# Order of declaration in a constant pool: the token rows ahead of the short vectors

## The chip, the cores and the metric

The kernel runs on one core of one Trainium2 chip. The metric is the device time of one execution in microseconds (us); lower is better. A core has five engines that work through their own instruction streams in order: TensorE (PE in the profile, with its weight loads shown apart as PEld), VectorE (DVE), ScalarE (ACT), GpSimd (POOL) and SyncE (SP, which here only starts DMA transfers). [...]

## The reference

A trunk of two layers over 512 tokens of width 1024 in float32. Each layer is a token mixer and a gated feed-forward block, each behind an RMS norm and added to the residual:

```python
for i in range(2):
    h = rms_norm(x, norm_mix[i])
    x = x + (mixer_a if i == 0 else mixer_b)(h, ...)
    h = rms_norm(x, norm_ffn[i])
    x = x + conv_ffn(h, f_w_up[i], f_conv_w[i], f_conv_b[i], f_w_down[i])
return rms_norm(x, norm_final)
```

`mixer_a` is a chunked causal gMLP (`gelu(h @ w_in)` split into u and v, v normed and mixed over the tokens of a chunk, `(u * v) @ w_out`); `mixer_b` a Griffin RG-LRU block (two projections, a short convolution, two gates, a linear recurrence, a projection out). `conv_ffn` is `(gelu(gate) * val) @ w_down` with `gate, val = split(causal_dwconv(h @ w_up))`, a convolution of width 3 over the tokens. The feed-forward width is 3072.

## The kernel before, in words

Everything is kept transposed: channels on the 128 partitions, the 512 tokens along the row. `xall` holds the residual x as 8 rows of 128 x 512 numbers (`xs[0]` to `xs[7]`). A product is made accurate by splitting both factors into a high and a low part of type fp32r. The gain-scaled x is kept so as `xh[0..7]` and `xl[0..7]`, eight tiles of 128 x 512 each (`norm_input`, L210 to L213); the weights are loaded in pieces of 128 x 1024 numbers (`raw`), and ScalarE makes the high part (L99), VectorE the low part (L100), each in a ring of three buffers of pool `wp`. One product is then three matmuls (`mm3`, L109 to L113): high by high, high weight by low x, low weight by high x.

In a TensorE matmul one factor of 128 x 128 is loaded first (the stationary one, a row of PEld) and the other, here 512 columns, streams past it (the moving one). The order in which the program runs, and what stands in each role:

- **v** (L374 to L376): four blocks of 96 matmuls. Here `xh` and `xl` are the stationary factor, 128 columns of them at a time, and the weights stream.
- **u** (four blocks of 96, the groups named `u` in the trace): the weights are stationary, `xh` and `xl` stream. In between stand the short matmuls `sv` that mix the tokens of a chunk.
- **aop** (384 matmuls): projection out of mixer A; the streaming factor is `ayh`/`ayl`, tiles of pool `yp`.
- **f** (12 blocks of 96 in each of two layers, named `f`, weights `fu...`): up-projection of the feed-forward block, `xh` and `xl` stream.
- **d** (L522): the first part of the down-projection by seven products of half size with 256 columns each; tiles `y` stream. In layer 0 twice 504 such matmuls, in layer 1 once, and there the rest is an ordinary projection (**fd**, L269 ff.), also over tiles `y`.
- **bx, bg** (three blocks of 96 each): `xh` and `xl` stream; in between stand the gate products **gt** (24 matmuls per head, streaming `xbh`/`xbl` of pool `yp`).
- **bop** (288 matmuls): projection out of mixer B, streaming `byh`/`byl` of pool `yp`.

So `xh` and `xl` are used in v, u, f, bx and bg, and in nothing else. The normalising factor of a token is not applied to x before the product but to the result: VectorE multiplies each finished 128 x 512 block by `rbc` (L545 in f, L448 in u, L631 and L642 in bx and bg). `acc` collects the squares for the norm (L221), TensorE sums it over the partitions (L232), and L246 spreads the factor over a 128 x 512 block that ScalarE copies to `rbc` (L247).

`vt` holds all short vectors (gains, convolution taps, biases) side by side, 536 columns; single columns of it are operands of ScalarE and VectorE instructions. The tiles of pool `const` get their addresses in the order in which they are declared, one behind the other, each size rounded up to 32 bytes. In the program that is built, `const` begins at byte 16512 of each partition, a multiple of 64, for `vt` takes 2144 bytes, which is 33 times 64 and 32 more: `xall` begins at byte 18656, 32 beyond a multiple of 64, and so do the sixteen tiles behind it (2048 bytes each). `acc` and `rbc`, declared at L203 and L204, begin at 69920 and 71968, 32 beyond a multiple of 64 too. Every tile of the other pools (weights, `ay`, `by`, `xb`, `y`, work tiles) begins on a multiple of 64.

The order of the work is set by a scheduler at build time, which gives each engine one fixed list; `tc.high_priority` (the weight splits and a few others) moves work ahead in it.

Of the kernel before, what the change touches and what calls it, by code (L numbers as in the profile page):

```python
# [8 lines left out]
F32 = mybir.dt.float32  # L9
# [5 lines left out]
P = 128  # L15
S = 512
# [24 lines left out]
NV = _off  # L41
# [3 lines left out]
def trunk(ctx: ExitStack, tc: tile.TileContext, xT, vecs, a_w_in, a_w_sT, a_b_s, a_w_out,  # L45
# [3 lines left out]
    const = ctx.enter_context(tc.tile_pool(name="const", bufs=1))  # L49
# [41 lines left out]
    def small(n, name):  # L91
        return const.tile([P, n], F32, name=name)
# [42 lines left out]
        return f  # L135


    vt = const.tile([P, NV], F32, name="vt")
    xall = const.tile([P, KD, S], F32, name="xall")
    xs = [xall[:, k, :] for k in range(KD)]  # L140
    xh = [const.tile([P, S], F32R, name=f"xh{k}") for k in range(KD)]
    xl = [const.tile([P, S], F32R, name=f"xl{k}") for k in range(KD)]
    xparts = list(zip(xh, xl))
    g0 = const.tile([P, KD], F32, name="g0")
    nc.scalar.dma_start(g0, vecs[:, _COLS["norm_mix"]:_COLS["norm_mix"] + KD])

# [53 lines left out]
        nc.vector.tensor_scalar(c4, u, LRU_C / 2, None, op0=ALU.mult)  # L200


    acc = const.tile([P, S], F32, name="acc")  # L203
    rbc = const.tile([P, S], F32, name="rbc")  # L204
    rc = small(NC, "rc")
    ms = small(NC, "ms")
    rch = const.tile([P, NC], F32R, name="rch")
# [560 lines left out]
```

## Time and profile before

| what | before |
|---|---|
| median of 3 runs | 1327.69 us (1327.13 to 1328.07) |
| the profiled execution | 1328.25 us, of which the span of the core is 1326.5 us |
| TensorE clock granted over the span | 0.998 of full speed |
| PE busy | 1316.4 us (99%), 6510 matmuls |
| PEld busy | 1103.5 us (83%) |
| DVE busy | 935.2 us (71%) |
| ACT busy | 600.6 us (45%) |
| POOL busy | 54.3 us (4%) |
| DMA | 143.47 MB, mean 108 GB/s |

"Busy" is the time in which an engine has at least one instruction under way. Matmuls overlap: the record of a 128 x 512 matmul is about 0.4 us long while the next one starts after 0.23 us, so what one costs in a stream is read from the distance of starts, not from its own length. The chain of waits is followed back from the last instruction: to whatever released each step, or to the instruction before it on its engine.

### The profile page before, as it was taken

How to read it: one execution, taken by the hardware profiler on the slowest of the kernel's cores; microseconds unless marked ns; L12 is line 12 of the kernel's file. 1: busy time of each engine (PE TensorE's matmuls, PEld its weight loads, DVE VectorE, ACT ScalarE, POOL GpSimd, SP SyncE). 2: the span in 40 equal slices, each digit the busy share in tenths (PEclk: the TensorE clock that was granted, in tenths of full speed). 3: DMA queues.
4: the chain of work that ended last, by engine and by line, in shares of the span. 5: the costliest groups of instructions: out<-in, count | busy, mean ns of one | idle time of the engine just before them, and what ended most of it. 6: DMA issues, size and time to landing. Idle time of an engine off the chain costs nothing.

```text
span 1326.5 us, 17029 instructions
## 1 busy us (share of the span) xinstructions
PE 1316.4 (99%) x6510; PEld 1103.5 (83%) x6510; DVE 935.2 (71%) x1336; ACT 600.6 (45%) x809; POOL 54.3 (4%) x56
## 2 busy tenths in 40 slices
PE   9999999999999999999999999999999999999997
PEld 7888888888888898888997888888888899888886
DVE  7227776446777877878987799954687788576735
ACT  6456333333444443444554669633344444343432
POOL 1000000000000120001200000000000012000000
PEclk9999999999999999999999999999999999999999
DMA  6333222232223574225752323233222357322221
GB/s 231 96 95 111 81 80 80 95 97 95 95 96 94 124 188 130 89 92 130 178 137 96 96 80 95 96 111 96 84 91 96 111 135 182 113 95 96 96 80 64
DMA packets 121105, 143.47 MB, mean 108 GB/s; under 512 B 7616, under 2 KB 95168, under 8 KB 121024
## 3 DMA queue, kind: packets, MB, share of 16 engines
q1 hardware_dynamic: 111088, 132.95, 31.5%
q0 software_dynamic: 9792, 9.44, 4.7%
q8 instruction: 51, 0.84, 0.3%
q14 instruction: 30, 0.25, 0.1%
q10 hardware_dynamic: 144, 0.00, 0.0%
HBM read 140.26 MB, written 2.10 MB: 107 GB/s over the span
## 4 chain that ended last, share of the span: by engine, by line
PE 99%; issue 1%; DVE 0%; DVEq 0%; POOLq 0%; POOL 0%
PE f L111 14%; PE f L112 14%; PE f L113 14%; PE v L374 2%; PE d000m L522 2%; PE d001m L522 2%; PE v L375 2%; PE u L111 2%; PE d101m L522 2%; PE d061m L522 2%; PE d100m L522 2%; PE d060m L522 2%; PE u L113 2%; PE u L112 2%; PE v L376 2%; PE aop L111 2%
## 5 line engine op out<-in xcount | busy, mean ns | idle before, releaser
L458 DVE SCALAR_TENSOR_TENSOR cv<-up,vt,cv 128x511 f32<-128x511 f32 x192 | 135.8, 745 | 0.7
L545 DVE TENSOR_TENSOR up<-f,rbc 128x512 f32<-128x512 f32 x96 | 63.7, 686 | 35.6 <-PE f L113 33.2
L456 ACT ACTIVATE cv<-up,vt 128x512 f32<-128x512 f32 x96 | 70.7, 804 | 0.5 <-DVE up L545 0.5
L561 ACT ACTIVATE cv<-cv 128x512 f32<-128x512 f32 x48 | 30.3, 632 | 34.4 <-DVE cv L458 34.3
L502 DVE TENSOR_TENSOR y<-yr,y 128x1792 fp32r<-128x1792 f32 x18 | 36.5, 2025 | 11.8 <-ACT y L501 11.8
L501 ACT CAST y<-yr 128x1792 fp32r<-128x1792 f32 x18 | 30.4, 1691 | 14.3 <-DVE yr L499 14.3
L226 POOL TENSOR_TENSOR rc<-ms,mhalf 128x4 f32<-128x4 f32 (+1 forms) x6 | 5.5, 912 | 665.2 <-DVE ms L225 665.2
L434 DVE SCALAR_TENSOR_TENSOR sv<-sv,vt,bs 128x256 f32<-128x256 f32 x32 | 15.0, 478 | 19.1 <-PE sv L431 19.1
L211 ACT ACTIVATE xh<-xall,vt 128x512 fp32r<-128x512 f32 x24 | 17.1, 717 | 20.3 <-DVE xall L263 15.8
L220 ACT ACTIVATE sq<-xall 128x512 f32<-128x512 f32 (+1 forms) x37 | 21.5, 586 | 9.8 <-DVE xall L275 9.8
L563 DVE TENSOR_TENSOR yr<-cv 128x512 f32<-128x512 f32 x36 | 24.7, 688 | 1.7
L458 DVE SCALAR_TENSOR_TENSOR xb<-xr,vt,xb 128x511 f32<-128x511 f32 (+2 forms) x36 | 25.5, 744 | 0.1
L221 DVE TENSOR_TENSOR acc<-acc,sq 128x512 f32<-128x512 f32 (+1 forms) x37 | 23.8, 642 | 2.0 <-ACT sq L220 1.9
L212 DVE SCALAR_TENSOR_TENSOR xl<-xall,vt,xh 128x512 fp32r<-128x512 f32 x24 | 17.8, 747 | 3.4 <-ACT xh L211 3.2
L430 PE MATMUL sv<-ws,vh 128*128 128x256 f32 x64 | 15.4, 324 | 0.0
L436 DVE SCALAR_TENSOR_TENSOR sv<-sv,vt 128x256 f32<-128x256 f32 x32 | 15.0, 479 | 0.4
L567 ACT CAST y<-cv 128x512 fp32r<-128x512 f32 x12 | 7.3, 617 | 16.1 <-DVE cv L565 16.1
L431 PE MATMUL sv<-ws,vl 128*128 128x128 f32 x64 | 14.2, 223 | 0.0
L698 DVE TENSOR_TENSOR_SCAN hs<-riyh,sq 128x512 f32<-128x512 f32 x12 | 14.0, 1207 | 0.0
L86 ACT ACT_TABLE_LOAD x10 | 12.8, 1283 | 0.1
L497 DVE TENSOR_TENSOR yr<-yr 128x512 f32<-128x512 f32 x18 | 12.5, 692 | 0.6
L431 PEld LDWEIGHTS sv<-ws,vl 128*128 128x128 f32 x64 | 12.3, 192 | 0.5
(2631 smaller groups left out, 4505.7 us busy)
## 6 DMA issues: line engine op xcount, KB each, us to landing
xall<-xT SPq DMA_DIRECT2D x8, 256.0 KB, 5.3
outT<-o SPq DMA_DIRECT2D x8, 256.0 KB, 2.2
av00raw<-a_w_in SPq DMA_DIRECT2D x2, 256.0 KB, 4.3
av01raw<-a_w_in SPq DMA_DIRECT2D x2, 256.0 KB, 5.6
av02raw<-a_w_in SPq DMA_DIRECT2D x2, 256.0 KB, 5.8
av03raw<-a_w_in SPq DMA_DIRECT2D x2, 256.0 KB, 4.8
bs<-a_b_s SPq DMA_DIRECT2D x1, 512.0 KB, 5.9
av10r<-a_w_in SPq DMA_DIRECT2D x1, 512.0 KB, 6.0
```

What stands on the lines that cost most here:

```text
L111: nc.tensor.matmul(ps, wh, xh, start=first, stop=False)
L112: nc.tensor.matmul(ps, wh, xl, start=False, stop=False)
L113: nc.tensor.matmul(ps, wl, xh, start=False, stop=last)
L374: nc.tensor.matmul(pss[c], xh[kk][:, ts], hi[:, k, :], start=kk == 0, stop=False)
L375: nc.tensor.matmul(pss[c], xh[kk][:, ts], lo[:, k, :], start=False, stop=False)
L456: nc.scalar.activation(dst, src, AF.Identity, scale=col(wname, woff + last * wstep), bias=col(cname, coff))
L458: nc.vector.scalar_tensor_tensor(dst[:, i:], src[:, :S - i], col(wname, woff + (last - i) * wstep), dst[:, i:], op0=ALU.mult, op1=ALU.add)
L501: nc.scalar.copy(hi, raw[:, 0:7])
L502: nc.vector.tensor_tensor(lo, raw[:, 0:7], hi.bitcast(F32), op=ALU.subtract)
L522: nc.tensor.matmul(banks[b][:, j], wt[:, w, js], xt, start=first and j == 0 and m == 0, stop=last and j == 1 and m == 2, skip_group_check= ...
L545: nc.vector.tensor_tensor(upt, pss[2 * half + j], rbc, op=ALU.mult)
L561: nc.scalar.activation(ts[0], ts[0], AF.Gelu_apprx_tanh)
```

## The change

Inside the constant pool, `vt` is declared behind the rows instead of ahead of them, and `acc` and `rbc` are declared with the rows instead of behind the small vectors. No instruction is added, removed or written otherwise.

```diff
-    vt = const.tile([P, NV], F32, name="vt")
+
     xall = const.tile([P, KD, S], F32, name="xall")
     xs = [xall[:, k, :] for k in range(KD)]
     xh = [const.tile([P, S], F32R, name=f"xh{k}") for k in range(KD)]
     xl = [const.tile([P, S], F32R, name=f"xl{k}") for k in range(KD)]
     xparts = list(zip(xh, xl))
+    acc = const.tile([P, S], F32, name="acc")
+    rbc = const.tile([P, S], F32, name="rbc")
+    vt = const.tile([P, NV], F32, name="vt")
     g0 = const.tile([P, KD], F32, name="g0")
...
-    acc = const.tile([P, S], F32, name="acc")
-    rbc = const.tile([P, S], F32, name="rbc")
     rc = small(NC, "rc")
```

In the built program the lists of instructions of all five engines are the same as before, row for row, with the same waits; only addresses differ:

| tile | byte in the partition, before | after |
|---|---|---|
| `xall` | 18656 = 291 x 64 + 32 | 16512 = 258 x 64 |
| `xh0` | 35040 = 547 x 64 + 32 | 32896 = 514 x 64 |
| `xl0` | 51424 = 803 x 64 + 32 | 49280 = 770 x 64 |
| `acc` | 69920 = 1092 x 64 + 32 | 65664 = 1026 x 64 |
| `rbc` | 71968 = 1124 x 64 + 32 | 67712 = 1058 x 64 |
| `vt` | 16512 = 258 x 64 | 69760 = 1090 x 64 |
| `ones`, the stationary factor of L246 | 68352 = 1068 x 64 | 72448 = 1132 x 64 |
| first tile of the next pool, `wp` | 74304 = 1161 x 64 | 74304, the same |

The other `xh` and `xl` follow in steps of 2048 bytes. From `rc` on, nothing moves.

## Rows read from the trace of the kernel before

**Rows 1.** The page: span, busy time by engine, the chain that ended last.
```profile
span 1326.5 us, 17029 instructions
PE 1316.4 (99%) x6510; PEld 1103.5 (83%) x6510; DVE 935.2 (71%) x1336; ACT 600.6 (45%) x809; POOL 54.3 (4%) x56
...
PE 99%; issue 1%; DVE 0%; DVEq 0%; POOLq 0%; POOL 0%
```

**Rows 2.** The waits, those of PE: waited for, us in total, times, longest us.
```profile
PE rb L298 <- DVE dg L291: 1.5, 1, 1.5
PE warm L158 <- DVE warm L155: 1.3, 1, 1.3
PE st L287 <- ACT sq L277: 1.0, 1, 1.0
```

**Rows 3.** Busy time of u, bg, f, v, bop, gt, from start to start.
```profile
core 0: us, PE busy (x) PEld busy (x) DVE busy (x) ACT busy (x) POOL busy (x), PEclk, DMA share, GB/s
97.45:119.94 22.49, 22.49 (x97) 18.11 (x96) 18.89 (x29) 17.91 (x32) 1.01 (x1) 1.00 0.36 113
829.24:851.73 22.49, 22.49 (x97) 18.11 (x96) 22.49 (x33) 13.70 (x19) 0.00 (x0) 1.00 0.28 95
940.86:963.35 22.49, 22.49 (x98) 18.12 (x96) 17.63 (x23) 9.86 (x11) 0.00 (x0) 1.00 0.29 94
52.65:75.05 22.40, 22.40 (x97) 18.03 (x96) 4.90 (x4) 9.63 (x17) 0.00 (x0) 1.00 0.29 93
851.73:917.03 65.30, 65.30 (x289) 54.10 (x288) 35.20 (x46) 25.83 (x35) 0.00 (x0) 1.00 0.32 105
801.46:806.90 5.44, 5.44 (x26) 4.51 (x24) 5.44 (x10) 5.41 (x8) 0.00 (x0) 1.00 0.39 103
```

**Rows 4.** Busy time over the span of the instructions with `xh`, then with `xl`.
```profile
0.00:1326.00 1326.00, 773.31 (x2432) 458.91 (x2432) 23.84 (x32) 22.84 (x32) 1.00 0.37 108
0.00:1326.00 1326.00, 481.99 (x1216) 229.37 (x1216) 23.84 (x32) 1.00 0.37 108
```

**Rows 5.** Groups by line, DVE and ACT, whole span: busy us, mean ns of one.
```profile
L545 DVE TENSOR_TENSOR up<-f,rbc 128x512 f32<-128x512 f32 x96 | 63.7, 686 | 35.6 <-PE f L113 33.2
L563 DVE TENSOR_TENSOR yr<-cv 128x512 f32<-128x512 f32 x36 | 24.7, 688 | 1.7
...
L212 DVE SCALAR_TENSOR_TENSOR xl<-xall,vt,xh 128x512 fp32r<-128x512 f32 x24 | 17.8, 747 | 3.4 <-ACT xh L211 3.2
L400 DVE SCALAR_TENSOR_TENSOR vl<-vr,rv,vh 128x512 fp32r<-128x512 f32 x16 | 10.9, 745 | 1.9 <-ACT vh L399 1.9
...
L399 ACT ACTIVATE vh<-vr,rv 128x512 fp32r<-128x512 f32 x16 | 10.1, 711 | 1.5 <-POOL rv L226 1.5
L211 ACT ACTIVATE xh<-xall,g 128x512 fp32r<-128x512 f32 x8 | 5.7, 715 | 2.2 <-DMA xall<-xT 1.1 <-DMA g<-vecs 1.0
```

**Rows 6.** One weight tile of an f block: its low part written (DVE), then loaded (PEld).
```profile
L113 PEld LDWEIGHTS f<-xh,fu122l x8: 187/188/193, 974.8 to 979.8; 128*128 128x128 f32 x8
L100 DVE TENSOR_TENSOR fu122l<-fu122r,fu122h x1: 1225/1225/1225, 964.4 to 964.4; 128x1024 fp32r<-128x1024 f32 x1
```

**Rows 7.** Busy time by stretch: the whole of the three bg blocks.
```profile
762.40:851.70 89.30, 89.30 (x385) 72.27 (x384) 88.67 (x128) 67.21 (x91) 0.00 (x0) 1.00 0.28 89
```

**Rows 8.** Timeline, PEld, in layer 0's first d stage and the first bg block.
```profile
455.38 0.19 PEld L522 LDWEIGHTS d000m<-y,d0001blo 128*128 128x128 f32 x1 [0.21 <-DVE d0001blo L483]
...
772.25 0.19 PEld L111 LDWEIGHTS gt<-xb4h,gw2h 128*128 128x128 f32 x1 [0.16 <-DVE xr L631]
```

**Rows 9.** Timeline, PE and DVE, in the first bx block and at the last one's end.
```profile
682.00 0.39 PE L111 MATMUL bx<-xh,bx00h 128*128 128x512 f32 x1
...
695.46 0.69 DVE L221 TENSOR_TENSOR acc<-acc,sq 128x512 f32<-128x512 f32 x1
...
696.51 0.28 PE L232 MATMUL st<-ones_f,acc 128*128 128x1 f32 x2
...
759.56 1.28 DVE L631 TENSOR_TENSOR xr<-bx,rbc 128x512 f32<-128x512 f32 x2
```

## The prediction

> **What bounds the kernel now.** I read the page first, for the engine that is the bound. TensorE is at work 99% of the span, and 99% of the chain that ended last is TensorE's [rows 1]. The waits come second: all of PE's add up to 3.8 us, and all three stand at the start or in the last 17 us [rows 2]. So between the first chunk and the tail, the time is the number of matmuls times the distance of their starts. The change takes no matmul away; it can only alter that distance, or the length of the work on VectorE and ScalarE beside it.
>
> So the third view is the distance in different stretches, each taken from the start of a first matmul to the start of the next stretch's first one, divided by the weight loads in it (one per matmul) [rows 3]:
>
> - one block each of u, bg and f, where `xh` and `xl` stream: 22.49 us / 96 = 234.3 ns in all three;
> - a block of v, where `xh` and `xl` are stationary and weights stream: 22.40 / 96 = 233.3 ns;
> - bop, streaming tiles of pool `yp`: 65.30 / 288 = 226.7 ns;
> - the gt of one head, inside a bg block, streaming such tiles: 5.44 / 24 = 226.7 ns.
>
> All are 128 x 512 with fp32r operands at a granted clock of 1.00, the 2.4 GHz level, where 512 columns take 213.3 ns. What the stretches at 233 and 234 ns share is `xh` or `xl`, which begin 32 bytes beyond a multiple of 64; every operand of the two at 226.7 ns begins on one. How busy the neighbours are does not sort them: v is at 233.3 ns with VectorE busy 4.90 of 22.40 us, gt at 226.7 ns with VectorE busy all of 5.44 us, and bg's own matmuls, with VectorE just as busy, at 234.3 ns [rows 3]. The surplus, 7.5 ns and 6.6 ns, is 18 and 16 columns at 2.4 GHz; 64 bytes hold 16 numbers. A row that starts off the boundary touching one more piece of 64 bytes would look like this. I take the address for the cause.
>
> **The change part by part.**
>
> *Streaming `xh` and `xl` on 64 bytes.* 2432 matmuls use `xh` and 1216 `xl`, 3648 in all [rows 4]; 4 x 96 = 384 are v's, so 3264 stream them: 2304 in f, 384 in u, 576 in bx and bg. Their price afterwards is not in the trace. Its ends are 234.3 ns (the address does nothing) and 226.7 ns (they become like bop). I take 226.7, as the same helper, shape and types run there. 3264 x 7.6 ns = 24.7 us (22.49/96 less 65.30/288, unrounded, is 7.54: 24.6 us).
>
> *Stationary `xh` and `xl` in v.* The ends are 0 and 384 x (233.3 - 226.7) = 2.5 us. I take 2.5: nothing but these operands is off the boundary in v either, and its surplus is nearly the same. This is the less certain term, as a weight load lies beside the matmul ahead of it.
>
> *`xall`, `acc`, `rbc` and `vt`, read and written by VectorE and ScalarE: nothing.* Pairs of rows with the same work differ by at most 4 ns, with either sign: with `rbc` off the boundary 686 ns, all on it 688; `xl` out of `xall` 747, `vl` 745; `xh` 715, `vh` 711 [rows 5]. Were the 4 ns real, the work would still lie beside TensorE, which is the bound. If that cover went, 96 x 4 ns for a group such as L545 would be 0.4 us.
>
> *What is given back.* The lists and waits stay, so an earlier TensorE can only run into what is late. In an f block VectorE works 17.63 us [rows 3], and a block would take 96 x 226.7 = 21.77 us: still room. A low weight part there is written by 965.6 and first loaded at 974.8, 9.2 us ahead [rows 6]; the whole gain of a block is 0.72 us. Four places are tight, two of them in the first bx block:
>
> - Layer 0's first d stage already waits for VectorE, 0.21 us [rows 8]. VectorE's chain of weight sums starts off buffers that TensorE frees in the f block ahead, so it moves along with TensorE; what TensorE can gain on it lies between nothing and the 0.72 us of that block. I take 0.2.
> - In the first bx block the last sum for the norm ends at 696.15, 0.36 us ahead of L232 [rows 9]. From the block's start at 682.00 to there stand some 60 matmuls, 0.45 us: 0.1 lost. The 12 matmuls from there to L246 lose another 0.1 us, for the chain over VectorE and GpSimd between has its own length.
> - In the first bg block, gt waits 0.16 us for VectorE to empty a bank of PSUM [rows 8], and VectorE works 88.67 of 89.30 us in the bg blocks [rows 7]. The emptying of those banks began at 759.56 [rows 9], 12.7 us earlier; they hold some 55 matmuls, 24 of them gt, so 31 of bg: up to 0.2 us.
>
> I take 0.6 us for all four; the ends are 0 and 2.2 us (VectorE holds TensorE to its own pace through all three bg blocks: 288 x 7.5 ns).
>
> *Sum.* 24.6 + 2.5 - 0.6 = 26.5 us. The profiled execution took 1328.25 us for a span of 1326.5, so it would take 1301.75. It stands 0.56 us above the median of the three runs, 1327.69; for the median that is **1301.2 us**.
>
> **The rivals.**
>
> 1. *Only the streaming operand counts.* Then v keeps its 233.3 ns for another reason (it alone has the roles exchanged). For: weight loads are 188 ns long [rows 6] and lie beside the running matmul. Against: the surplus is 16 columns, as in f. The sum loses 2.5 us: 1303.7 us.
>
> 2. *VectorE takes over in the second half.* In bx and bg the 576 matmuls of these blocks would gain 4.3 us, but VectorE has 0.63 us of idle time in the bg blocks [rows 7]. If it is the bound from the last bx block on, 2.2 us (bg) to 4.3 us (bx and bg) of the gain are lost: 1303.4 to 1305.5 us. Against: PE has no wait in these blocks that the list of waits counts [rows 2], and the one in the timeline is 0.16 us [rows 8]; in the last of them, with VectorE at work all the time, TensorE still runs at 234.3 ns [rows 3].
>
> 3. *The address does nothing.* What sets `xh` and `xl` apart is then something else that moves with them unchanged (that they are written by ScalarE and VectorE at the end of a stage, or read by five stages). The distances stay at 234.3 and 233.3 ns and the time at 1327.7 us. Against: `ayh`, `byh` and `xbh` are written in the same way, by one ScalarE and one VectorE instruction each. The Trainium skill has a rule that speaks for this rival: "SBUF — State Buffer", section "Specifications (TRN2)", gives lines of 16 bytes as the unit in which reads pay for crossing over. By that, a row that starts 32 bytes beyond a multiple of 64 starts on a line as well as after the change, and the sum would be 0. By that rule, v, f, u, bx and bg should run as bop does, and the rows disagree by 6.6 and 7.5 ns.
>
> 4. *Slower: the neighbours pay.* TensorE's streams, VectorE and ScalarE now all begin in the same phase of 64 bytes, and VectorE's instructions in the f blocks become longer because they meet TensorE's reads. The place is VectorE in f: it decides from 22.49 / 17.63, 28% longer instructions, on; at 30% a block takes 22.9 us, 24 blocks lose 24 x 0.43 = 10 us, and the time is 1338 us. Against: L563, with all its operands on the boundary, takes 688 ns in the same stage, L545 686 [rows 5].
>
> **How the numbers follow.** About 0.2% (2.7 us) is what a measurement of this kernel can tell from no change. My forecast gets 0.77, rival 1 0.09, rival 2 0.06, rival 3 0.05, rival 4 0.03. Forecast and rivals 1 and 2 are faster by over 1.6%: faster 0.92, same 0.05, slower 0.03. The forecast's own range runs from 1300.6 (all of 27.1 us, nothing given back) to 1302.8 (all of 2.2 given back); the runs of before spread by 0.9 us, so the low end is 1299.8. For the high end, rivals 1 and 2 belong in, up to 1305.5 and the spread: 1306. Rivals 3 and 4, 0.08, are left out.
>
> **What would show it.** Right: blocks of f, u, bx and bg of 21.8 us and of v of 21.8 us, bop unchanged at 65.3; the d stages, fd and the tail as long as before; instructions of VectorE and ScalarE of the same length. TensorE's busy time falls with the span and its share stays at 99%. Blocks of v at 22.4 show rival 1. New waits of PE for VectorE in bg, or bg blocks longer than those of f by more than their gt, show rival 2. Blocks of f at 22.5 show rival 3 and make the prediction wrong, as would an L545 longer than its 686 ns by a fifth.

## The result, and the profile after

| | before | after |
|---|---|---|
| median, runs of one chip | 1327.76 us (1327.13 to 1328.07, 4 runs) | 1311.65 us (1311.40 to 1314.92, 4 runs) |
| ratio | | 0.9885, 95% interval 0.9868 to 0.9902 |
| the profiled execution | 1328.25 us, span 1326.5 | 1311.40 us, span 1309.7 |

Faster, by 16.1 us, where 26.5 us were forecast and 1306 us was the high end of the range. The sign was right; 10.4 us of the gain are missing. The page of the profile after, against [rows 1]:

```profile
span 1309.7 us, 17029 instructions
PE 1299.0 (99%) x6510; PEld 1100.3 (84%) x6510; DVE 934.5 (71%) x1336; ACT 600.8 (46%) x809; POOL 54.3 (4%) x56
...
PE 98%; issue 1%; DMA 0%; DVE 0%; ACT 0%; DVEq 0%; POOLq 0%; POOL 0%
```

PE's busy time fell by 17.4 us and the span by 16.8; VectorE and ScalarE work as long as before, within 0.7 us. TensorE is still the bound. So the gain did not run into another engine: the matmuls themselves gained less than forecast. Their distance stands in the same stretches as in [rows 3], in the same order (u, bg, f, v, bop, gt; columns as there):

```profile
core 0: us, PE busy (x) PEld busy (x) DVE busy (x) ACT busy (x) POOL busy (x), PEclk, DMA share, GB/s
96.72:119.12 22.40, 22.40 (x97) 18.16 (x96) 18.89 (x29) 17.81 (x32) 1.01 (x1) 1.00 0.36 112
818.45:840.42 21.97, 21.97 (x97) 18.04 (x96) 21.97 (x32) 13.65 (x19) 0.00 (x0) 1.00 0.30 97
929.14:951.12 21.98, 21.98 (x98) 18.04 (x96) 17.64 (x23) 9.90 (x11) 0.00 (x0) 1.00 0.30 96
51.92:74.33 22.41, 22.41 (x98) 17.96 (x97) 4.90 (x4) 9.62 (x17) 0.00 (x0) 1.00 0.31 93
840.42:905.75 65.33, 65.33 (x289) 54.08 (x288) 36.41 (x48) 25.84 (x35) 0.00 (x0) 1.00 0.32 105
790.96:796.45 5.49, 5.49 (x26) 4.51 (x24) 5.49 (x10) 5.46 (x8) 0.00 (x0) 1.00 0.36 99
```

f and bg went from 234.3 to 228.9 ns (21.97 / 96), this block of u only to 233.3, and v stayed at 233.4. None reached the 226.7 ns of bop (65.33 / 288 = 226.8), though all their operands now begin on 64 bytes. The gt shown takes 0.05 us more than before: by the trace its first ten matmuls, right behind those of bg, start 224 to 236 ns apart, the others every 226.7 ns. The clock is 1.00 in all of them.

By the starts of the stages, the 16.8 us between the two spans (16.9 before rounding) lie as follows: 0.7 ahead of u, 1.4 from u's start to aop's, 0.0 in aop, 6.7 from layer 0's first f block to bx (12 blocks of f at 0.51 us are 6.1 of it), 1.2 in bx with the gt between, 1.4 in bg, and 5.6 from bop's start to the end (again 12 blocks of f, less 0.5 us that the stretch from fd's start to the end is longer, 78.3 us after 77.8). The 0.7 us ahead of u are no gain of v's stream: they lie in v's first block, where the program starts up (24.1 us before, 23.4 after); the other three blocks take 22.95, 22.40 and 22.40 us in both kernels.

The waits of PE are those of [rows 2] and one more, in v's beginning; the lines of VectorE and ScalarE last as long as in [rows 5]:

```profile
PE rb L299 <- DVE dg L292: 1.5, 1, 1.5
PE warm L161 <- DVE warm L158: 1.3, 1, 1.3
PE st L288 <- ACT sq L278: 1.0, 1, 1.0
PE v L375 <- ACT av00hi L356: 0.6, 1, 0.6
```

```profile
L546 DVE TENSOR_TENSOR up<-f,rbc 128x512 f32<-128x512 f32 x96 | 63.6, 686 | 32.8 <-PE f L113 31.0
L564 DVE TENSOR_TENSOR yr<-cv 128x512 f32<-128x512 f32 x36 | 24.7, 687 | 1.7
...
L213 DVE SCALAR_TENSOR_TENSOR xl<-xall,vt,xh 128x512 fp32r<-128x512 f32 x24 | 17.8, 746 | 3.4 <-ACT xh L212 3.2
```

One more view says what sort of thing the missing time is. The timeline after, PE, grouped by weight tile, in u's second block and in an f block: smallest, median and largest length in ns, then the starts of the first and the last one in us. The lengths are modelled, but from matmul to matmul their differences are clear:

```profile
L111 PE MATMUL u<-xh,au10h x8: 397/398/398, 119.1 to 124.0; 128*128 128x512 f32 x8
L112 PE MATMUL u<-xl,au10h x8: 397/398/398, 119.4 to 124.3; 128*128 128x512 f32 x8
L113 PE MATMUL u<-xh,au10l x8: 397/398/398, 119.6 to 124.5; 128*128 128x512 f32 x8
L111 PE MATMUL u<-xh,au11h x8: 393/394/448, 125.6 to 130.5; 128*128 128x512 f32 x8
L112 PE MATMUL u<-xl,au11h x8: 388/388/397, 125.9 to 130.7; 128*128 128x512 f32 x8
L113 PE MATMUL u<-xh,au11l x8: 392/392/393, 126.1 to 130.9; 128*128 128x512 f32 x8
...
L111 PE MATMUL f<-xh,fu111h x8: 394/394/395, 934.6 to 939.4; 128*128 128x512 f32 x8
L112 PE MATMUL f<-xl,fu111h x8: 388/388/389, 934.9 to 939.7; 128*128 128x512 f32 x8
L113 PE MATMUL f<-xh,fu111l x8: 392/392/392, 935.1 to 939.9; 128*128 128x512 f32 x8
```

Up to 124.5 us every matmul is long, in u's first block too. Then the short `sv` matmuls come in between, and from 125.6 us on the same stream, over the same addresses, has a pattern of three, which the blocks of f have too. So a row that begins on 64 bytes doesn't settle the pace by itself: something beside it does, and it can stand in more than one state.

### The profile page after: what moved, and what is told of

Same layout as the page of the kernel before. It is cut to its first block, busy times and chain, and to the rows that moved or that the text cites. A ratio compares the mean times of both kernels' runs of the same rounds, so it can differ in the third digit from the quotient of the medians.

```text
span 1309.7 us, 17029 instructions
## 1 busy us (share of the span) xinstructions
PE 1299.0 (99%) x6510; PEld 1100.3 (84%) x6510; DVE 934.5 (71%) x1336; ACT 600.8 (46%) x809; POOL 54.3 (4%) x56
## 4 chain that ended last, share of the span: by engine, by line
PE 98%; issue 1%; DMA 0%; DVE 0%; ACT 0%; DVEq 0%; POOLq 0%; POOL 0%
PE f L111 14%; PE f L112 13%; PE f L113 13%; PE v L375 2%; PE d101m L523 2%; PE d061m L523 2%; PE d001m L523 2%; PE d100m L523 2%; PE d000m L523 2%; PE d060m L523 2%; PE v L376 2%; PE u L111 2%; PE v L377 2%; PE u L112 2%; PE u L113 2%; PE aop L111 2%
## 5 line engine op out<-in xcount | busy, mean ns | idle before, releaser
L546 DVE TENSOR_TENSOR up<-f,rbc 128x512 f32<-128x512 f32 x96 | 63.6, 686 | 32.8 <-PE f L113 31.0
L564 DVE TENSOR_TENSOR yr<-cv 128x512 f32<-128x512 f32 x36 | 24.7, 687 | 1.7
L213 DVE SCALAR_TENSOR_TENSOR xl<-xall,vt,xh 128x512 fp32r<-128x512 f32 x24 | 17.8, 746 | 3.4 <-ACT xh L212 3.2
L432 PEld LDWEIGHTS sv<-ws,vl 128*128 128x128 f32 x64 | 12.2, 191 | 0.5
```

What stands on the lines that cost most here:

```text
L432: nc.tensor.matmul(ps[:, i, 1], vl[:, ds_], w[:, 0], start=False, stop=True)
L546: nc.vector.tensor_tensor(upt, pss[2 * half + j], rbc, op=ALU.mult)
```

## The experiments

While one matmul runs, TensorE loads the weights of the one behind it: PEld works 1100.3 us beside PE's 1299.0. So it reads two rows at one time out of SBUF, the on-chip memory in whose partitions all these tiles lie: the streaming factor and, for the matmul behind it, the stationary one. From this comes the theory that I formed from the trace after: **D** in the texts on record says that the **distance** between the starts of these two decides, whatever either start is by itself. bop and gt had distance 0 by chance: their pool `yp` and the weights' `wp` both begin 64 bytes beyond a multiple of 256. The other letters are rivals, with what each asks for beside them. All four of the first runs let the rows and the weights begin at the same place, modulo 256, by tiles that nothing reads. No instruction that computes or loads is changed in any kernel of this section; e9 and e11 have one more wait on ScalarE than the others (17030 instructions for 17029).

### Rows and pools moved together: four ways to distance 0

```diff
 e1, against the kernel after
+    pad0 = const.tile([P, 16], F32, name="pad0")
     xall = const.tile([P, KD, S], F32, name="xall")
...
+    pad1 = const.tile([P, 16], F32, name="pad1")
     vt = const.tile([P, NV], F32, name="vt")
 e2, against the kernel after: rows where they are, everything from wp on 64 bytes later
     vsum = small(NC * 4, "vsum")
+    pad1 = const.tile([P, 16], F32, name="pad1")
 e3, against the kernel before: everything from wp on 160 bytes later
     vsum = small(NC * 4, "vsum")
+    pad1 = const.tile([P, 40], F32, name="pad1")
 e4, against the kernel before: xh and xl, and wp with them, moved
     xall = const.tile([P, KD, S], F32, name="xall")
...
+    pad0 = const.tile([P, 56], F32, name="pad0")
     xh = [const.tile([P, S], F32R, name=f"xh{k}") for k in range(KD)]
...
+    pad1 = const.tile([P, 40], F32, name="pad1")
```

> The changed kernel with 64 empty bytes ahead of xall and 64 behind rbc. All rows and all tiles of the other pools then begin 64 bytes beyond a multiple of 128; in the changed kernel the rows begin on a multiple of 128 and the other pools 64 beyond one. Theory D (what counts is the distance, modulo 128 bytes, between the streaming row and the weights loaded beside it; at distance 0, as bop and aop have it, a matmul starts every 226.7 ns): f, bx, bg, u and v all fall to 226.7 ns. From the changed kernel's 228.9 ns in f, bx and bg (2880 matmuls, 6.4 us), 233.3 in v (384, 2.5 us) and 230 to 233 in u (384, 1.8 us) that is some 10.7 us less: 1301 us. Theory B (a row start on 64 bytes is all that counts, and what is left above 226.7 ns has another cause): 1311.6 us, f at 228.9, v at 233.3.

> The changed kernel with 64 empty bytes at the end of the constant pool: the rows stay on a multiple of 128, and all other pools now begin on one too. Distance 0 again, from the other side. Theory D: as the run before, 1301 us, all 128 x 512 matmuls at 226.7 ns. Theory B: 1311.6 us. A third theory, A (the place of the rows or of the weights counts by itself, 64 beyond 128 being good and 0 bad): here xh, ay, by and the weights all begin on 128, so bop and aop would get slower than 226.7 ns and the time would go above 1311.6 us.

> The kernel before with 160 empty bytes at the end of the constant pool: the rows stay 32 bytes beyond a multiple of 64, and so do now all tiles of the other pools, weights, ay, by, xb and y included. Distance 0, but nothing on 64. Theory D: 226.7 ns everywhere, about 1301 us. Theory B: nothing gained in f, u, v, bx and bg (234.3 and 233.3 ns), and aop, bop, gt and fd lose 7 ns on each of some 1060 matmuls, 7 us more: 1335 us, and more still if the 256-column matmuls of d pay too.

> The kernel before with 224 empty bytes between xall and xh0 and 160 behind g0: xh and xl begin at distance 0 from the weights (64 beyond a multiple of 128), while xall, acc and rbc stay 32 beyond a multiple of 64 as before. If only TensorE's operands count: 1301 us under theory D, 1311.6 under B, with VectorE's and ScalarE's instructions as long as before (686 and 715 ns). If the rows that VectorE and ScalarE read count as well, the time stays above that of the first run of this group by what their instructions lose.

| | `xh`, `xl` / weights / pools `yp`, `y`, modulo 256 | median us (runs) | ratio, 95% interval |
|---|---|---|---|
| e1 | 192 / 192 / 192 | 1302.51 (1301.34 to 1303.27, 4) | 0.9814, 0.9799 to 0.9828 |
| e2 | 128 / 128 / 128 | 1301.29 (1301.05 to 1302.22, 4) | 0.9805, 0.9788 to 0.9821 |
| e3 | 224 / 224 / 224 | 1302.65 (1301.16 to 1303.87, 4) | 0.9815, 0.9800 to 0.9830 |
| e4 | 192 / 192 / 192 | 1301.68 (1301.55 to 1301.99, 4) | 0.9808, 0.9794 to 0.9823 |

The kernel before took 1326.98 us beside them. The time by stretch, f and v in e1; f, v, bop and half a d stage in e2; f and bop in e3; f in e4:

```profile
922.85:944.61 21.76, 21.76 (x97) 18.02 (x96) 17.63 (x23) 10.00 (x11) 0.00 (x0) 1.00 0.30 97
51.45:73.22 21.77, 21.77 (x98) 18.02 (x97) 4.90 (x4) 9.52 (x17) 0.00 (x0) 1.00 0.31 93
```

```profile
922.36:944.12 21.76, 21.76 (x98) 18.02 (x97) 17.63 (x23) 9.99 (x11) 0.00 (x0) 1.00 0.31 97
51.19:72.95 21.76, 21.76 (x97) 18.02 (x96) 4.90 (x4) 9.50 (x17) 0.00 (x0) 1.00 0.30 94
833.83:899.11 65.28, 65.28 (x290) 54.05 (x288) 37.03 (x48) 26.24 (x36) 0.00 (x0) 1.00 0.32 105
637.95:668.19 30.24, 30.24 (x255) 30.24 (x253) 27.21 (x45) 17.79 (x28) 4.77 (x4) 1.00 0.67 167
```

```profile
921.05:942.81 21.76, 21.76 (x97) 18.02 (x96) 17.63 (x23) 10.00 (x11) 0.00 (x0) 1.00 0.30 97
832.61:897.88 65.27, 65.27 (x289) 54.05 (x288) 37.02 (x48) 26.25 (x36) 0.00 (x0) 1.00 0.32 105
```

```profile
921.64:943.40 21.76, 21.76 (x97) 18.02 (x96) 17.63 (x23) 10.00 (x11) 0.00 (x0) 1.00 0.30 97
```

21.76 / 96 = 226.7 ns in f and v alike, in all four. e3 decides: there no `xh`, no `xl` and no weight begins on 64 bytes, and bop, which left its boundary, lost nothing. e2 differs from the kernel after by 64 bytes ahead of the pools, its rows lie where they lay, and it gains 25.7 us of the 26.5 that were forecast. So at distance 0 the start of a row by itself does nothing, and of the theories D is the one that stands. In e4 `xall` (224), `acc` and `rbc` (160) lie off 64 bytes, and the time is that of the others: VectorE and ScalarE don't ask for it. The pattern of three is gone as well. The timeline of e2, PE, the same f block:

```profile
L111 PE MATMUL f<-xh,fu111h x8: 389/389/389, 927.8 to 932.6; 128*128 128x512 f32 x8
L112 PE MATMUL f<-xl,fu111h x8: 389/389/389, 928.0 to 932.8; 128*128 128x512 f32 x8
L113 PE MATMUL f<-xh,fu111l x8: 389/389/389, 928.2 to 933.0; 128*128 128x512 f32 x8
```

### The kernel after once more

Is the pattern, and the change from one state to the other, the same in another execution (Q), or drawn anew in each (P)? The kernel after, unchanged.

> The changed kernel itself, once more, with a second profile. In the first profile the same stream at the same addresses ran at two paces: u at 233.3 ns until the first sv matmuls, then about 231; bx at 233.3 until the norm's matmuls in its first block, then 228.9. One of the four times was 1314.92 us, the others 1311.4 to 1311.7. Theory P (at distance 64 a stream has two paces, 228.9 and 233.3 ns, and falls into one or the other when it is interrupted): the times again differ by more than those of the kernels at distance 0 do for their waits, and the second profile shows at least one f, u, bx or bg stretch at another pace than the first. Theory Q (the pace goes with the place in the program alone): the second profile has the same paces at the same places, and the times stay within 1 us of 1311.6.

1311.48 us (1311.38 to 1314.18, 4 runs; before 1327.21), ratio 0.9885 (0.9870 to 0.9899). Its profile, u's first block and an f block:

```profile
96.70:119.10 22.40, 22.40 (x97) 18.14 (x96) 18.89 (x29) 17.81 (x32) 1.01 (x1) 1.00 0.36 114
929.76:951.73 21.97, 21.97 (x97) 18.03 (x96) 17.64 (x23) 9.89 (x11) 0.00 (x0) 1.00 0.30 96
```

Both as in the first profile, at the same places: the two profiles agree, as Q asks. Its other sign, times within 1 us of 1311.6, was missed by one run, which took 2.7 us more than the others, as one of the first four took 3.2 us more; neither has a profile, so what they did stays open.

### High and low weights at two distances

In the kernel after, the rings of `wp` are laid out by hand, so that the high parts stay 64 bytes off and the low parts, which meet `xh` alone, go to distance 128:

```diff
+    for tag, n in (("raw", 1024), ("hi", 1024), ("pa", 16), ("lo", 1024), ("pb", 16)):
+        wp.tile([P, n], F32, tag=tag, name=f"first{tag}")
```

> The changed kernel with 64 bytes (three buffers, 192 in all) between the rings of high and low weights and as many behind the low ones. Rows xh, xl on a multiple of 128, high weights 64 beyond one, low weights on one, ay, by, xb and y 64 beyond one. Theory D says which loads meet which stream: in f, u, bx and bg the loads of high weights are at distance 64, those of low weights at 0; in aop, bop, gt and fd it is the other way round. So both kinds should lie between 226.7 ns and the changed kernel's pace: f above 226.7, and bop and aop, which stood at 226.7 in every run so far though nothing was done to them, above 226.7 too. If only where the rows begin mattered, bop and aop would stay at 226.7 and f at 228.9 or 233.3. If the distance of low and high weights does nothing at all, likewise.

1320.85 us (1320.29 to 1320.90, 3 runs), ratio 0.9949 (0.9933 to 0.9964): 9 us worse than the kernel after. Two blocks of f (one of a layer's first seven, one of its last five), one of v, and bop of its profile:

```profile
935.81:958.00 22.19, 22.19 (x98) 18.03 (x97) 17.64 (x23) 9.87 (x11) 0.00 (x0) 1.00 0.30 95
1150.76:1173.23 22.47, 22.47 (x98) 18.09 (x96) 15.34 (x21) 9.22 (x12) 0.00 (x0) 1.00 0.30 94
51.75:73.72 21.97, 21.97 (x97) 18.03 (x96) 4.90 (x4) 9.53 (x17) 0.00 (x0) 1.00 0.31 95
845.85:912.10 66.25, 66.25 (x289) 54.04 (x288) 35.30 (x46) 25.79 (x35) 0.00 (x0) 1.00 0.31 104
```

f went from 228.9 to 231.1 ns in the first block shown and to 234.1 in the second; a block each of u, bx and bg takes 22.45 to 22.49 us, 233.9 to 234.3 ns. bop, whose rows now lie at 192 with high weights at 64 and low ones at 0, went from 226.8 to 230.0: its pace in the kernel before was no property of bop, as D asks. The range that the text gives was missed, as it ends at the 228.9 ns of the kernel after. It counts distances modulo 128, by which the low weights would stand at 0 from `xh`; modulo 256, which the next runs call for, they stand at 128.

### Which distance, and by which modulus

Two kernels after e1's pattern, with other sizes:

```diff
 e7, against the kernel after: pad0 of 16 columns, pad1 of 48
 e8, against the kernel after: pad0 of 8 columns, pad1 of 24
+    pad0 = const.tile([P, 16], F32, name="pad0")
     xall = const.tile([P, KD, S], F32, name="xall")
...
+    pad1 = const.tile([P, 48], F32, name="pad1")
     vt = const.tile([P, NV], F32, name="vt")
```

The texts of the runs so far and that of e8 count distances modulo 128. Modulo 256, which these runs then call for, e8's rows (160) stand 224 from its weights (192), and those of the kernel before (224 and 64) stood 160 from theirs.

> The changed kernel with 64 empty bytes ahead of xall and 192 behind rbc: rows 192 beyond a multiple of 256, weights and other pools 64 beyond one, so the distance is 128. If the distance counts modulo 128: 226.7 ns everywhere, 1301 to 1302.5 us. If it counts modulo 256 or more: the matmuls of f, u, v, bx and bg stay above 226.7 ns and the time is up to 1311.6 us or more.

> The changed kernel with 32 empty bytes ahead of xall and 96 behind rbc: rows 32 beyond a multiple of 128, weights 64 beyond one, distance 96 (the kernel before had 32). Theory D with a collision by pieces of 64 bytes: as the kernel before or a little different, f between 228.9 and 234.3 ns or more, 1315 to 1328 us. Theory B (rows off 64): 1327 us.

e7: 1323.08 us (1322.83 to 1323.55, 6 runs), ratio 0.9967 (0.9955 to 0.9980). e8: 1324.64 us (1323.81 to 1325.17, 10 runs), 0.9980 (0.9971 to 0.9989). Two blocks of f (again one of a layer's first seven and one of its last five), v and bop of e7, then f and v of e8:

```profile
936.73:959.13 22.40, 22.40 (x98) 18.02 (x96) 17.64 (x23) 9.87 (x11) 0.00 (x0) 1.00 0.30 94
1153.90:1176.21 22.31, 22.31 (x97) 18.09 (x96) 15.36 (x21) 9.21 (x12) 0.00 (x0) 1.00 0.30 95
52.40:74.70 22.30, 22.30 (x98) 18.08 (x96) 4.90 (x4) 9.58 (x17) 0.00 (x0) 1.00 0.30 92
847.72:913.01 65.29, 65.29 (x289) 54.05 (x288) 35.47 (x46) 25.85 (x35) 0.00 (x0) 1.00 0.31 105
```

```profile
938.22:960.62 22.40, 22.40 (x98) 18.03 (x96) 17.64 (x23) 9.86 (x11) 0.00 (x0) 1.00 0.29 94
52.61:75.01 22.40, 22.40 (x98) 17.99 (x97) 4.90 (x4) 9.60 (x17) 0.00 (x0) 1.00 0.30 93
```

At a distance of 128 f runs at 233.3 ns in the first block shown and at 232.4 in the second, so 128 is not as good as 0, and the modulus is not 128. In e7 every row begins on 64 bytes, as in the kernel after, and yet it gains only 4.1 us on the kernel before (1327.21): the same alignment, 64 bytes further on, is worth a quarter of what the change brought.

To part 256 from 512, and to see the other streams at other distances, e9 and e10 start from the kernel after with pads in three places:

```diff
 e9: 80, 96, 48 columns; e10: 16, 48, 112 columns
     vsum = small(NC * 4, "vsum")
+    pad1 = const.tile([P, 80], F32, name="pad1")
...
-        stack = enter(("y", 6), ("yr", 1), ("sm", 1), ("wk", 8))
+        stack = enter(("py", 1), ("y", 6), ("yr", 1), ("sm", 1), ("wk", 8))
+        phase["py"].tile([P, 96], F32, name="pady")
...
-    mixer = enter(("yp", 24), ("wk", 7))
+    mixer = enter(("pz", 1), ("yp", 24), ("wk", 7))
+    phase["pz"].tile([P, 48], F32, name="padz")
```

> The changed kernel with empty bytes in three places, so that the streaming rows begin at three distances from the weights, modulo 512 (the step of the weight columns): xh and xl at 256 (320 bytes at the end of the constant pool), xbh, byh and byl at 192 (a tile of 192 bytes ahead of pool yp in the second mixer), y at 384 (a tile of 384 ahead of pool y). ay stays at 0. Theory D256 (the distance counts modulo 256): u, f, bx and bg at 226.7 ns, v too. Theory D512: they stay above, at 228 to 234. Both: bop and gt leave 226.7 ns for 228 to 234, and so does fd, though nothing but an empty tile ahead of their pool is added; aop stays. Theory B (only a start on 64 bytes counts): nothing moves against the changed kernel. For the 256-column matmuls of d, at 120.0 ns in all kernels but e6, where they took 117.8 with y at 384 from the high and 192 from the low weights: if 384 is what did it, 117.8 or less.

> As the run beside it, with xh and xl at distance 0 (64 bytes at the end of the constant pool), xbh, byh and byl at 448, y at 192. u, f, bx, bg and v at 226.7 ns. bop and gt at 228 to 234. fd above 226.7. d at 117.8 ns or less if 192 is what did it in e6, else at 120 or above.

e9: 1305.70 us (1305.65 and 1305.74), ratio 0.9835 (0.9806 to 0.9863). e10: 1302.74 us (1301.64 and 1303.83), 0.9812 (0.9784 to 0.9841). f, bop and a gt of e9, then bop and half a d stage of e10:

```profile
924.79:946.55 21.76, 21.76 (x97) 18.02 (x96) 17.64 (x23) 10.00 (x11) 0.00 (x0) 1.00 0.31 97
834.39:901.59 67.20, 67.20 (x290) 53.86 (x288) 36.77 (x49) 25.78 (x35) 0.00 (x0) 1.00 0.31 102
785.07:790.67 5.60, 5.60 (x26) 4.49 (x24) 5.60 (x11) 5.57 (x8) 0.00 (x0) 1.00 0.35 97
```

```profile
833.93:901.13 67.20, 67.20 (x289) 53.87 (x288) 36.78 (x48) 25.77 (x35) 0.00 (x0) 1.00 0.31 102
637.95:667.45 29.50, 29.50 (x254) 29.48 (x253) 27.69 (x46) 17.54 (x28) 4.77 (x4) 1.00 0.70 177
```

In e9 the weights lie 256 bytes from the rows, modulo 512, and f runs at 226.7 ns: the modulus is 256. bop and gt, the steady ones so far but for e6, run at 233.3 ns (67.20 / 288, 5.60 / 24) as soon as their pool stands 192 off the weights. So does fd, which had 226.7 ns, with `y` at 128 (e9) and at 192 (e10). The whole of it, for a matmul of 512 columns (distance: streaming less stationary, modulo 256):

| distance | ns from start to start | where |
|---|---|---|
| 0 | 226.7 | bop, gt before; u, f, v, bx, bg, bop and gt in e1 to e4 |
| 32 | 233.3 | v in e8 |
| 64 | 228.9, or 233.3 | f, bg after; u's first block and the start of bx after |
| 96 | 233.3 | v before |
| 128 | 233.3, or 232.3 | f in e7, fd in e9; u, v, bx's first blocks and a layer's last five blocks of f in e7 |
| 160 | 234.3 | f, u, bx, bg before |
| 192 | 233.3 | v after; bop, gt in e9 and e10 |
| 224 | 233.3 | f in e8 |

Distance 0 was seen with the rows at four places (64, 128, 192 and 224, modulo 256) and 128 at three. Each of the others was seen with a single pair of places, so there the distance and the places are not told apart. Nor do the runs tell whether the weights being loaded count or those in use: except in e6, both begin at the same place, modulo 256.

### A version that beats both

The half-size products of d, with 256 columns, are not at their best at distance 0: half a d stage of 252 matmuls takes 30.24 us in e2 (120.0 ns each) and 29.50 us in e10 (117.1), where `y` stands 192 off. At 128, in e9, it takes 30.24 as well. So: e2, with `y` alone at 192. e2 itself runs beside it, as e12.

```diff
 e11, against e2
-        stack = enter(("y", 6), ("yr", 1), ("sm", 1), ("wk", 8))
+        stack = enter(("py", 1), ("y", 6), ("yr", 1), ("sm", 1), ("wk", 8))
+        phase["py"].tile([P, 48], F32, name="pady")
```

> e2 (rows at distance 0, all else on the same place) with a tile of 192 bytes ahead of pool y alone. u, f, v, bx, bg, aop, bop and gt at 226.7 ns; fd at 233.3 (240 matmuls, 1.6 us lost against e2); d at 113.3 to 117.8 ns where nothing else holds it up, 2.2 to 6.7 ns less on 1512 matmuls, 3.4 to 10 us, of which VectorE's weight sums take back what they need: the matmuls of d wait for them already in e10 (d060 at 125.4 ns a matmul with its waits, d061 at 117.1). Out of e10's 1302.74 us less 432 x 6.6 ns for bop and gt: 1299.9 us, 1.4 us under e2. If the waits take all of it back: 1301 to 1303.

> e2 once more, on the same chip as e11, for the difference of the two: 1301.3 us, f, bx, bg, u and v at 226.7 ns, d at 120.0.

e11: 1299.00 us (1298.40 to 1299.73, 5 runs), ratio 0.9785 (0.9772 to 0.9799). e12: 1302.48 us (1300.99 to 1303.14, 4 runs), 0.9809 (0.9796 to 0.9822). The runs of the two don't overlap: 3.5 us between the medians. f, bop and half a d stage of e11:

```profile
919.59:941.35 21.76, 21.76 (x97) 18.02 (x96) 17.63 (x23) 10.00 (x11) 0.00 (x0) 1.00 0.30 97
831.09:896.37 65.28, 65.28 (x290) 54.05 (x289) 37.07 (x48) 26.28 (x36) 0.00 (x0) 1.00 0.33 105
636.06:665.56 29.50, 29.50 (x255) 29.49 (x254) 27.77 (x46) 17.56 (x28) 4.77 (x4) 1.00 0.70 169
```

Over all 1512 matmuls of d, waits included, the traces give a mean distance of 117.2 ns in e11, 121.1 in e12 and 120.5 in e2: 4.9 to 5.9 us less. The ordinary projection fd over the same `y` gives back 1.6 us, as its 512 columns want distance 0: its 240 matmuls of that shape take 54.40 us in e12 and 56.00 in e11 (233.3 ns each). e11 is 28.7 us faster than the kernel before, 12.6 us faster than the change.

## Why the prediction was right or wrong

**The bound: right.** TensorE's stream of matmuls is what the change moved, and PE's busy time fell with the span (17.4 and 16.8 us).

**Streaming, 24.6 us: wrong in its price.** The step that failed is "I take 226.7, as the same helper, shape and types run there". It took bop's pace for the pace of rows on 64 bytes. By the blocks shown, f's 2304 matmuls gained 5.3 ns each instead of 7.5 (12.2 us of 17.4), bg's last block the same (1.6 us for three such blocks; the whole stretch with its gt gained 1.4), and u's first block 1.0 ns. The cause behind it was wrong too. "Every operand of the two at 226.7 ns begins on one" was true, and so was that those operands begin at the same place, modulo 256, as the weights loaded beside them; the one was taken for the other. What decides in its place is the distance of the two rows: 64 in the kernel after, which costs 228.9 or 233.3 ns, and 0 in e1 to e4, which costs 226.7 with the rows on 64 bytes or off them. The rows read could have told them apart no further, as all the pools stood at 64; the table of addresses in the section on the change could have raised the question, since the change puts `xh` at 128, modulo 256, and leaves `wp` at 64. That a boundary shared by both operands is also a distance of theirs was the rival that wasn't on the list.

**Stationary rows in v, 2.5 us: wrong, measured 0** (22.40 before, 22.41 after). Rival 1 foresaw the number, but not the reason: it said that the stationary operand doesn't count, and in e1 to e4 v falls to 226.7 ns as all the others do. In the change, v only went from a distance of 96 to one of 192, which cost the same.

**VectorE and ScalarE, nothing: right.** L546 (before L545) 686 ns, L564 687, L213 746; and e4, with `xall`, `acc` and `rbc` off the boundary, is as quick as e2.

**Given back, 0.6 us: neither shown nor needed.** After the start of the program no wait of PE came that wasn't there before, but the gain that was to be given back from was smaller too. With the full gain, e2 waits 0.5 us for VectorE in d, where 0.2 was taken. The forecast's sum as a whole is met by the kernels at distance 0, 1301.3 to 1302.7 us against 1301.2: the size of the surplus and what it costs were read rightly, and only what takes it away was not. These kernels spread by up to 2.7 us from run to run, against at most 1.7 of before (16 runs); that VectorE is late at one d stage or another in each run is likely, but only argued.

**Rival 2 (VectorE takes over): no.** VectorE works all of a bg block, 21.97 us, and the block is no longer than one of f. In e1 to e4, with blocks still shorter, it adds no more than the waits above.

**Rival 3 (the address does nothing): no.** Only addresses were changed, and the time fell by 16.1 us. True in it is that the boundary of 64 bytes does nothing by itself, as e3 shows at distance 0. The rule of the Trainium skill named there ("SBUF — State Buffer", "Specifications (TRN2)", lines of 16 bytes) does not account for the paces: every row in these kernels begins on a line, and their matmuls start 226.7 to 234.3 ns apart. Another page of the Trainium skill bears on what was found: "TensorE: Matmul & The Clock Gate", "Step-by-step: what each phase is for", gives TensorE two independent ports to SBUF, by which loading the next weights doesn't take reading bandwidth from the running matmul. The traces disagree in the small: where the loaded rows begin, against the streaming ones, is worth up to 7.6 ns of a matmul. By which means is not shown.

**Rival 4 (the neighbours pay): no**, by the same lines as above.

## What to carry to other kernels

A group of rows that shares the good pace usually shares more than one property: before an address is priced, write down the addresses of all operands that the engine reads at the same time, as differences and by several moduli, and look which differences also sort the rows. In a TensorE-bound kernel of fp32r matmuls, let the streaming tiles begin at the same place modulo 256 bytes as the weights loaded beside them; a dead tile of 64 bytes at the end of a pool does it, and was worth 9 to 10 us more than the change here (e12 and e2). Then look at each shape by itself, as 256 columns want another distance than 512.

## What the runs showed of the hardware that was not expected

- The pace of a matmul of 512 columns depends on the distance between its two operands, modulo 256 bytes: 226.7 ns at 0, with the rows at four places; 232.3 or 233.3 at 128, with the rows at three; 228.9 to 234.3 at the six other multiples of 32, each tried with one pair of places. The usual surplus, 233.3 less 226.7, is 6.7 ns, or 16 columns at 2.4 GHz, which are 64 bytes. 228.9 is a third of that above 226.7, and goes with a pattern of three matmuls.
- One stream over the same addresses can run at two paces: at distance 64, u's first block at 233.3 ns until other matmuls came between, then with the pattern of f. In two executions it happened at the same place. At distance 128 (e7) f has 233.3 ns in most of a layer's first seven blocks and 232.4 in those behind the d stage; in e6 it has 231.1 ns and 234.1 in the same two stretches. What sets the state is open.
- The distances don't add up simply: in e6, with high weights at 64 and low ones at 128, f ran at 231.1 to 234.1 ns, and v, whose two distances cost 233.3 and 232.3 ns when alone, at 228.9 ns; bop, with 128 and 192, ran at 230.0. Why the modulus is 256, and why 256 columns are quicker at 192 (117.1 ns on average) than at 0 (120.0), is open as well.
